# A hybrid diffusion layer on one core: last filter weights made at the modulation, bias frames moved, 24 convolution phases ahead of the attention

## The chip, the cores and the metric

The kernel runs on one core of a Trainium2 chip. The metric is the device time of one launch in microseconds (us): the median of several runs, and beside it one execution that the hardware profiler took, with its own time. The names of the engines are those of the profile: PE is TensorE (matmuls; PEld its weight loads), DVE is VectorE, ACT is ScalarE, POOL is GpSimd, and SP is SyncE, which here issues transfers only. Each engine, and each queue of transfers, works strictly in the order in which its instructions were written down.

## The reference

One layer is applied to 256 context tokens and 1024 latent tokens (a grid of 16 rows by 64) of width 1024, all in float32. Cut to what matters:

```python
h = _rmsnorm(x, norm1_g) * (1.0 + sc1) + sh1            # modulation, sc/sh from silu(c) @ w_ada + b_ada
proj = h @ w_in                                          # 1024 -> 3072 columns
q, k, v = heads(proj[..., :1536])                        # 8 heads of 64
hy = _dwconv3(proj[..., 1536:], hy_conv_w, hy_conv_b)    # three groups x1, x2, v of 512 channels
a = attend(q, k, v)                                      # latent: 8x16 neighbourhood + bias, and 256 context keys
z = x1 * _long_conv(v, k_f[:, 0], filt_bias[0])          # FFT convolutions, order 2
hyo = x2 * _long_conv(z, k_f[:, 1], filt_bias[1])
merged = concat(_rmsnorm(a, g_a), _rmsnorm(hyo, g_h))
x = x + g1 * (merged @ w_out)
u = _dwconv3(h2 @ w_up, ffn_conv_w, ffn_conv_b)          # then silu(gate) * up, @ w_down, residual, final norm
```

The filters of the long convolutions are themselves the output of a small network, whose last step is what the change touches:

```python
h = jnp.sin(freq * (z @ w1 + b1))
h = jnp.sin(freq * (h @ w2 + b2))
h = (h @ w3 + b3).reshape(L, HY_ORDER, 2, HY_CH)         # order, forward/backward, 512 channels
h = h * jnp.exp(-t[:, None] * deltas[None, :])[:, None, None, :]
k_f = rfft(concat(fwd, zeros, flip(bwd[1:])))
```

Outputs are the two token streams after the final norm and the context's keys and values.

## The kernel before

Products that need float32 accuracy are made of three matmuls (`mm3`, L115 to L118): each operand is split into a rounded high part (ACT, L121) and the rest (POOL, L122), and high x high, low x high and high x low are summed in PSUM. The program is written as Python that issues instructions; a scheduler sorts them by priority (normally the place where they are written) and by its own estimates, once, when the program is built. What runs is then fixed: one list for each engine and each queue. `tc.high_priority(offset=2000)` lets instructions compete as if written 2000 instructions earlier; `tc.issue_after(x)` forbids that a transfer or instruction is listed before x.

The stages, in the order of time:

1. **Modulation** (to 79 us). `filter_hidden` (L289) runs the two sine layers of the filter network. `adaln` (L210) streams the weights of scale and shift (tiles `wada`) through TensorE. Then, for three groups of tokens (`gi` 0, 1, 2: four, four and two tiles of 128 rows), tiles `x` are normalised (L511 to L514), transposed by TensorE (L267), scaled by ScalarE into `mo` (L269, L272), and split by VectorE into the high and low halves `hh` and `hl` (L274, L275), which stay in SBUF. The first query projection is made in the same loop, with its product in the PSUM tag `fA` (L533).
2. **Projections and filters** (80 to 560 us). 23 projections of 128 columns each (`proj`, L616) load a weight tile `wr` through SP (L606), split it and multiply it with all 1280 tokens into the PSUM tag `psp`. Twelve of them (`hy_chunk`, L652) feed the convolution and store transformed-ready tiles to DRAM (`lxd`, `cxd`); eleven (`qkv`, L682) feed the attention. Between their matmuls lie those of `filters` (L371): for each of the two orders, four blocks of 128 channels (`lat_filter`, L423) and the context's filter (`ctx_filter`, L470). One such block multiplies the hidden layer with the last weights (L376, PSUM tag `fB`), multiplies by the decays of ScalarE (`dec`, L380), corrects the first row with the filter bias (`fix0`, L382; its small load `fb`, L385, has one buffer), adds and subtracts on POOL (L394, L395), splits on ACT and DVE (L397, L399), transforms by `mm3` into `fA`, and stores to `Kd` or `Kc` in DRAM (L467, L489).
   The last weights of one order come from `w3load(o)` (L345): two loads of raw rows one after the other through the same buffer `csl0`, sums and differences into the buffer `cs0`, which the filters also use, and a split into `ws[0]` and `ws[1]`. It runs once in front of each order.
   `rpb_frames` (L550) makes one of three frames of the attention's position bias: 16 small transfers issued by POOL, a copy, a store to `rpw` in DRAM. The three are written behind the first three of the query, key and value projections (`j == 0`, L755).
3. **Convolution** (458 to 834 us). `chain(j)` (L772) convolves channel block j in two orders (j = 4 is the context). Each order has four *phases*, divided by `yield`: the forward transform (TensorE L805 into PSUM `cA`, ACT L813 to L818, DVE L819); butterflies and the product with the filter `K` loaded from `Kd` (DVE L826 to L847); inverse butterflies (DVE L852 to L857, ACT L862 and L863, DVE L864); and the inverse transform (TensorE L877, DVE L882 to L890). Two *lanes* run alternately, j = 0, 2, 4 in one and j = 1, 3 in the other, 40 turns in all (`turn2`, L903). The first 16 are written ahead of the attention, with three PSUM banks; the others are written into the attention, with one bank. The convolution uses the SBUF space of the filters, so it cannot begin before these are done.
4. **Attention** (598 to 866 us). POOL loads queries and keys of a head pair (`qkload`, L970), bias tables (`bias_load`, L958: 16 transfers from `rpw` for each of three tables `tb`) and values `vs` (L1044). `scores` (L1061) makes score products in PSUM `psS` (L1058), adds the bias and takes the maximum on DVE (L1079), and exponentiates on ACT (L1092, L1093). Then TensorE transposes the probabilities (L1102), ACT and DVE evict them (L1008, L1006), and TensorE multiplies with the values (L1016).
5. **Output projection, feed-forward** (from 866 us). The output weights `wor` are loaded and split (L1187, L1188) as soon as the convolution's buffers are free.

## Time and profile before

| | before |
|---|---|
| median of 3 runs | 1855.13 us (1854.43 to 1856.17) |
| the profiled execution: its own time | 1859.47 us |
| its span, first to last instruction | 1857.7 us |
| granted TensorE clock, mean | 0.962 |
| PE busy | 1723.9 us, 93% |
| DVE busy | 1368.3 us, 74% |
| ACT busy | 892.5 us, 48% |
| POOL busy | 396.3 us, 21% |

An engine's busy time is the union of its instructions. A row of a timeline gives the start and the length in us, engine, source line, operation, what is written and read, and in brackets how long the engine had been idle and what ended that. A row of busy time by stretch gives, for a stretch of the span, each engine's busy time with the number of its instructions. Matmuls overlap in TensorE's pipeline, so the distance from start to start, and not the length of one, tells how fast they follow each other. Lines below are those of the kernel before; in the changed kernel the lines behind L342 stand 6 to 18 lower.

### The profile page before, as it was taken

Reading aid. Unit: us, or ns where it says so; the run is one execution under the profiler, and the core shown is the slowest. Engines: PE = TensorE matmul, PEld = TensorE weight load, DVE = VectorE, ACT = ScalarE, POOL = GpSimd, SP = SyncE. Lnnn points to the kernel's source line nnn. Section 1 sums busy time; section 2 is a strip of 40 time slices with the busy share of each in tenths; the row PEclk is TensorE's granted clock in tenths of the full one; section 3 lists DMA queues with packets and bytes.
Section 4 is the critical chain, followed back from the end, with each engine's and each line's share of the span. In section 5 each row is a group of like instructions: output and inputs, shape, how many; then the busy total and the mean of one; then the engine's idle time right before and its main releaser. Section 6 shows DMA issues by size and latency. Waiting matters only on the chain.

```text
span 1857.7 us, 27350 instructions
## 1 busy us (share of the span) xinstructions
PE 1723.9 (93%) x9999; PEld 1453.9 (78%) x9999; DVE 1368.3 (74%) x2166; ACT 892.5 (48%) x1852; POOL 396.3 (21%) x487
## 2 busy tenths in 40 slices
PE   5899999999994689897998899999999999999997
PEld 1688778788783355465886899999999999788786
DVE  4668957861878789873467888889777877556797
ACT  4755545533333576664555444444444444443452
POOL 2366656673018325500110000000000000000001
PEclk7999999999996799898998999999999999999999
DMA  7424354356445323514331444555222122934653
GB/s 265 146 75 142 112 168 131 110 149 211 145 137 160 102 80 102 140 44 144 119 106 65 147 157 146 172 176 165 76 68 67 56 74 96 342 120 136 205 189 130
DMA packets 202438, 249.76 MB, mean 134 GB/s; under 512 B 21922, under 2 KB 147987, under 8 KB 202049
## 3 DMA queue, kind: packets, MB, share of 16 engines
q1 hardware_dynamic: 190360, 230.75, 38.5%
q0 software_dynamic: 10240, 16.46, 3.7%
q8 instruction: 78, 1.28, 0.3%
q10 hardware_dynamic: 1705, 0.82, 0.2%
q14 instruction: 55, 0.45, 0.1%
HBM read 176.75 MB, written 71.20 MB: 133 GB/s over the span
## 4 chain that ended last, share of the span: by engine, by line
PE 54%; DVE 19%; DMA 13%; ACT 5%; issue 5%; POOL 3%; SPq 0%; DVEq 0%; ACTq 0%; POOLq 0%
PE psd L116 5%; PE psd L117 5%; PE psd L118 5%; PE psp L116 4%; PE psp L118 4%; PE psp L117 4%; DMA wt<-in_w_down_dram 3%; PE psa L116 2%; PE psa L117 2%; PE psa L118 2%; DMA tdr<-wt 2%; PE psc L118 2%; PE psc L117 2%; PE psc L116 2%; PE psb L117 1%
## 5 line engine op out<-in xcount | busy, mean ns | idle before, releaser
L116 PE MATMUL psp<-hh,wh 128*128 128x512 f32 (+1 forms) x552 | 200.7, 364 | 1.9 <-ACT wh L121 1.9
L117 PE MATMUL psp<-hl,wh 128*128 128x512 f32 (+1 forms) x552 | 199.0, 361 | 0.0
L118 PE MATMUL psp<-hh,wl 128*128 128x512 f32 (+1 forms) x552 | 199.0, 361 | 0.0
L1737 POOL TENSOR_TENSOR rs<-rs,mhalf 128x1 f32<-128x1 f32 x10 | 7.7, 775 | 816.4 <-DVE rs L1736 816.4
L116 PE MATMUL psa<-T,ws 128*128 128x256 f32 (+1 forms) x528 | 165.8, 314 | 3.8 <-ACT rows L1536 2.7
L117 PE MATMUL psa<-T,ws 128*128 128x256 f32 (+1 forms) x528 | 165.1, 313 | 0.0
L118 PE MATMUL psa<-T,ws 128*128 128x256 f32 (+1 forms) x528 | 164.6, 312 | 0.0
L116 PE MATMUL psd<-wd,gs 128*128 128x512 f32 x360 | 140.7, 392 | 3.6 <-ACT gs L121 3.6
L117 PE MATMUL psd<-wd,gs 128*128 128x512 f32 x360 | 141.0, 392 | 0.0
L118 PE MATMUL psd<-wd,gs 128*128 128x512 f32 x360 | 123.8, 391 | 2.0 <-DVE gs L122 2.0
L116 PEld LDWEIGHTS psp<-hh,wh 128*128 128x128 f32 x552 | 104.9, 190 | 23.2 <-issue 7.4
L118 PEld LDWEIGHTS psp<-hh,wl 128*128 128x128 f32 x552 | 104.6, 189 | 15.3 <-issue 1.2
L117 PEld LDWEIGHTS psp<-hl,wh 128*128 128x128 f32 x552 | 104.9, 190 | 14.0 <-issue 0.4
L116 PE MATMUL psc<-T,ws 128*128 128x384 f32 (+1 forms) x352 | 110.0, 313 | 6.0 <-ACT ws L121 6.0
L967 POOL DMA_DIRECT2D tb<-rpw x192 | 100.3, 530 | 58.0 <-DVE m L1079 24.3
L117 PE MATMUL psc<-T,ws 128*128 128x384 f32 (+1 forms) x352 | 110.1, 313 | 0.0
L118 PE MATMUL psc<-T,ws 128*128 128x384 f32 (+1 forms) x352 | 109.7, 312 | 0.0
L117 PE MATMUL psb<-T,ws 128*128 128x384 f32 (+1 forms) x352 | 109.4, 311 | 0.0
L118 PE MATMUL psb<-T,ws 128*128 128x384 f32 (+1 forms) x352 | 109.4, 311 | 0.0
L116 PE MATMUL psb<-T,ws 128*128 128x384 f32 (+1 forms) x352 | 109.2, 310 | 0.0
L116 PEld LDWEIGHTS psa<-T,ws 128*128 128x128 f32 x528 | 101.3, 192 | 5.5 <-ACT rows L1536 3.9
L117 PEld LDWEIGHTS psa<-T,ws 128*128 128x128 f32 x528 | 101.3, 192 | 0.0
(404 smaller groups left out, 4783.9 us busy)
## 6 DMA issues: line engine op xcount, KB each, us to landing
wada<-in_w_ada_dram SPq DMA_DIRECT2D x48, 512.0 KB
wr<-in_w_up_dram SPq DMA_DIRECT2D x44, 512.0 KB
gr<-gdr SPq DMA_DIRECT2D x44, 320.0 KB
wr<-in_w_in_dram SPq DMA_DIRECT2D x23, 512.0 KB
wt<-in_w_down_dram SPq DMA_DIRECT2D x44, 256.0 KB
tdr<-wt SPq DMA_DIRECT2D x44, 256.0 KB
gdr<-cv SPq DMA_DIRECT2D x22, 512.0 KB
wr<-tdr SPq DMA_DIRECT2D x20, 512.0 KB
```

The costliest lines, as they stand in the source:

```text
L116: T.matmul(out, ah, bh, start=start, stop=False, skip_group_check=True)
L117: T.matmul(out, ah, bl, start=False, stop=False, skip_group_check=True)
L118: T.matmul(out, al, bh, start=False, stop=stop, skip_group_check=True)
L967: blast[0] = G.dma_start(out=tv[:, :, a * 8:a * 8 + 64], in_=rpw[var, :, 2 * p_:2 * p_ + 2, :, d * 8:d * 8 + 64].rearrange("q h u x -> q ( ...
L1737: G.tensor_tensor(rs, rs, mhalf, op=ALU.pow)
```

## The change

Five edits. `w3load(o)` is written for both orders inside the modulation, when the group `gi == 1` has its loads, together with the transform's table `dft`, `dlt` and `nt`, which stood behind the first `hy_chunk`; both halves of the raw rows get their own buffer, the difference moves from DVE to POOL, and POOL's results go straight to the rounded tiles, without a cast. The second order's pair is stored to DRAM (`W3d`) and loaded back in front of its filters. The bias frames move from `j == 0` to `j == 2`. The number of phases written ahead of the attention goes from 16 to 24. And the first loads of the attention get a forced order: first table, values, then the zeroing of the probability buffers and the other two tables.

```diff
-    W3GO = ()
     XW = (1,)
+    W3d = dr.tile([2, P, 1024], F32, name="W3d")
 
     def w3load(o):
+        cs = slice(o * 1024, (o + 1) * 1024)
+        raw = [ft([P, 2, 512], f"csl{i}") for i in range(2)]
+        w3 = I["filt_w3"][0, :, cs]
+        V.memset(raw[1][64:128], 0.0)
+        for i, q in ((0, 0), (0, 64), (1, 0)):
+            Q.dma_start(out=raw[i][q:q + 64].rearrange(f2), in_=w3)
+        for q in (64, 96):
+            Q.dma_start(out=raw[1][q:q + 1].rearrange(f2), in_=I["filt_b3"][0:1, cs])
+        s = ft([P, 2, 512], "csh0")
+        ws0 = ft([P, 2, 512], "GE" if o else "ws0", F32R)
+        for r, t in zip(raw, (ws0, s)):
+            G.tensor_add(t[:, 0], r[:, 0], r[:, 1])
+            G.tensor_sub(t[:, 1], r[:, 0], r[:, 1])
+        rd = ft([P, 2, 512], "csh1", F32R)
+        A.copy(rd, s)
+        ws1 = ft([P, 2, 512], "csl0" if o else "ws1", F32R)
+        G.tensor_sub(ws1, s, rd.bitcast(F32))
+        A.copy(ws1[64:96], rd[64:96].bitcast(F32))
+        if o:
+            for i, w in enumerate((ws0, ws1)):
+                Q.dma_start(out=W3d[i], in_=w.bitcast(F32).rearrange(f2))
+        return ws0, ws1
+
+    def w3again():
         ws = [ft([P, 2, 512], f"ws{i}", F32R) for i in range(2)]
...
+        for i, w in enumerate(ws):
+            Q.dma_start(out=w.bitcast(F32).rearrange(f2), in_=W3d[i])
         return ws
...
             if o:
-                Ws = w3load(o)
+                Ws = w3again()
...
                 with tc.issue_after(wlast) if gi else ExitStack():
-                    Q.dma_start(out=x, in_=src[0, row * P:(row + 1) * P])
+                    xlast = Q.dma_start(out=x, in_=src[0, row * P:(row + 1) * P]).ins
...
+            if gi == 1:
+
+                with tc.issue_after(xlast):
+                    t = ft([P, 512], "sd00")
+                    Q.dma_start(out=t, in_=I["t_dft"].flatten().rearrange("(p x) -> p x", p=P))
+                    split(t, dft[0].rearrange(f2), dft[1].rearrange(f2))
+                    Q.dma_start(out=dlt, in_=I["t_delta"])
+                    Q.dma_start(out=nt, in_=I["t_nt"])
+                    Ws0 = w3load(0)
+                    w3load(1)
...
             if j + which == 0:
...
-                with tc.issue_after(wloads[-1]):
-                    Ws0 = w3load(0)
                 filters(hs1, hs2, Ws0)
...
-            if j == 0:
+            if j == 2:
                 rpb_frames(ip.tile([P, LT], F32, tag="fo", name="rp", bufs=1), which)
...
     with tc.high_priority(offset=CHP):
-        phases(16)
+        phases(24)
...
     first = qkload(0)
-    for var in range(3):
-        G.memset(tbs[var], NEG)
-        bias_load(0, var)
-        if var == 0:
-            for r in Pring:
-                for t in r:
-                    G.memset(t[:, 0, :, 11:16], 0.0)
-                    G.memset(t[:, 1, :, 0:4], 0.0)
+    G.memset(tbs[0], NEG)
+    bias_load(0, 0)
+    with tc.issue_after(blast[0]):
+        vfirst, vlast = vload(0)
+    with tc.issue_after(vlast):
+        for r in Pring:
+            for t in r:
+                G.memset(t[:, 0, :, 11:16], 0.0)
+                G.memset(t[:, 1, :, 0:4], 0.0)
+        for var in (1, 2):
+            G.memset(tbs[var], NEG)
+            with tc.issue_after(blast[0]):
+                bias_load(0, var)
```

`vload` holds the three value loads that stood in `attend`, word for word.

How the scheduler moves the rest, at three places. First ACT at the end of the modulation, up to the cast of the first projection weights (`wh<-wr`); before:

```order
L269 ACTIVATE mo<-pstB,mods,A_79 128x256
L269 ACTIVATE mo<-psp,mods,A_79 128x256 x2
L272 ACTIVATE hh<-psp,mods,A_79 128x256
L269 ACTIVATE mo<-psp,mods,A_79 128x256
L269 ACTIVATE mo<-pstB,mods,A_79 128x256
L540 COPY tm<-psfA 128x256
L542 DMA qd<-tm 128x256
L121 CAST wh<-wr 128x1024
```

and in the changed kernel (`dec` are the filters' decays, `csh` the split of their sums, L423 the scaling behind their transform):

```order
L403 CAST csh_1011<-cs_1008 128x1024
L269 ACTIVATE mo<-psp,mods,A_79 128x256 x2
L272 ACTIVATE hh<-psp,mods,A_79 128x256
L386 ACTIVATE dec<-dlt,nt 128x128 x6
L269 ACTIVATE mo<-psp,mods,A_79 128x256
L386 ACTIVATE dec<-dlt,nt 128x128 x2
L269 ACTIVATE mo<-pstB,mods,A_79 128x256
L556 COPY tm<-psfA 128x256
L423 ACTIVATE tm<-psfA,tw 128x128 x2
L558 DMA qd<-tm 128x256
L121 CAST wh<-wr 128x1024
```

The filters of the first channel blocks have moved in between the modulation's own instructions, ahead of the first projection.

Second SP, the queue of the loads, at the same place; `fb` is the small filter bias, `wr` a projection's weights. Before:

```order
L221 DMA wada_0_2643<-in_w_ada_dram 128x1024
L216 DMA mr_2639<-in_b_ada_dram 4x256 x2
L606 DMA wr<-in_w_in_dram 128x8x128
L353 DMA csl_874<-in_filt_w_dram 64x1024
L744 DMA tm<-in_t_dft_dram 128x512
L355 DMA csl_874<-in_filt_w_dram 64x1024
L606 DMA wr<-in_w_in_dram 128x8x128 x2
```

and now:

```order
L368 DMA W3d<-GE 128x1024
L221 DMA wada_0_2646<-in_w_ada_dram 128x1024
L216 DMA mr_2642<-in_b_ada_dram 4x256 x2
L391 DMA fb<-in_filt_bias_dram 1x128
L368 DMA W3d<-csl_561 128x1024
L391 DMA fb<-in_filt_bias_dram 1x128 x2
L622 DMA wr<-in_w_in_dram 128x8x128 x5
```

The projections' weights now stand behind the stores of the second order's pair and behind three filter biases, the last of them that of the fourth channel block.

Third DVE at the first score (an ISA row is the maximum with bias, L1079 before and L1097 now). Before, these rows of the convolution stand just ahead of it:

```order
L826 TENSOR_TENSOR s_6035<-s_5773 128x1024
L864 SCALAR_TENSOR_TENSOR s_5623<-s_5623,tw,t 128x2x128
L827 TENSOR_TENSOR s_5773<-s_5773 128x4x256
L830 TENSOR_TENSOR s_6036<-s_6035 128x4x128
L831 TENSOR_TENSOR s_6036<-s_6035 128x4x128
L1079 ISA Pl_5833,m_5950<-psS,tb_5857 128x3x88
```

and now:

```order
L852 TENSOR_TENSOR s_6276<-s_6267,K 128x1024
L853 TENSOR_TENSOR s_6008<-s_6267,K 128x1024
L890 TENSOR_TENSOR tt<-pscA,s_6245 128x512
L891 TENSOR_TENSOR tt<-pscA,s_6245 128x512
L854 TENSOR_TENSOR s_6008<-s_6008,s_6276 128x512
L855 TENSOR_TENSOR s_6008<-s_6008,s_6276 128x512
L1097 ISA Pl_6068,m_6185<-psS,tb_6092 128x3x88
```

The convolution's lines stand 8 lower in the changed kernel, so L852 here is L844 of before. 155 of its instructions stood ahead of the first score on VectorE; now it is 240.

More of the change, by code (lines that the diff above doesn't have):

```diff
@@ L340, in _build @@
     f2 = "p a b -> p (a b)"
-    W3GO = ()
     XW = (1,)
+    W3d = dr.tile([2, P, 1024], F32, name="W3d")
     def w3load(o):
-        ws = [ft([P, 2, 512], f"ws{i}", F32R) for i in range(2)]
-        cs = slice(o * 1024, (o + 1) * 1024)
-        raw = ft([P, 2, 2, 512], "GO") if o in W3GO else None
-        for i in range(2):
-            r = raw[:, i] if o in W3GO else ft([P, 2, 512], "csl0")
-            s = ft([P, 2, 512], "cs0")
-            Q.dma_start(out=r[0:64].rearrange(f2), in_=I["filt_w3"][0, :, cs])
-            if i == 0:
-                Q.dma_start(out=r[64:128].rearrange(f2), in_=I["filt_w3"][0, :, cs])
-            else:
-                V.memset(r[64:128], 0.0)
-                for q in (64, 96):
-                    Q.dma_start(out=r[q:q + 1].rearrange(f2), in_=I["filt_b3"][0:1, cs])
-            G.tensor_add(s[:, 0], r[:, 0], r[:, 1])
-            V.tensor_sub(s[:, 1], r[:, 0], r[:, 1])
-            if i == 0:
-                A.copy(ws[0], s)
-            else:
-                rd = ft([P, 2, 512], "csh1" if o in W3GO else "csh0", F32R)
-                A.copy(rd, s)
-                G.tensor_sub(ws[1], s, rd.bitcast(F32))
-                A.copy(ws[1][64:96], rd[64:96].bitcast(F32))
@@ L740, in _build @@
             if j + which == 0:
-                t = ft([P, 512], "tm", bufs=2)
-                e = "p a b -> p (a b)"
-                Q.dma_start(out=t, in_=I["t_dft"].flatten().rearrange("(p x) -> p x", p=P))
-                split(t, dft[0].rearrange(e), dft[1].rearrange(e))
-                Q.dma_start(out=dlt, in_=I["t_delta"])
-                Q.dma_start(out=nt, in_=I["t_nt"])
-                with tc.issue_after(wloads[-1]):
-                    Ws0 = w3load(0)
                 filters(hs1, hs2, Ws0)
@@ L968, in bias_load, with vload @@
                     var, :, 2 * p_:2 * p_ + 2, :, d * 8:d * 8 + 64].rearrange("q h u x -> q (h u) x")).ins
+    def vload(p_):
+        vs = tp.tile([P, 12, P], F32, tag="vs", name="vs", bufs=2)
+        G.dma_start(out=vs[:, 0:10], in_=vd[:, :, p_ * P:(p_ + 1) * P].rearrange("n p x -> p n x"))
+        for h in range(2):
+            ld = G.dma_start(out=vs[:, 10:12, h * DH:(h + 1) * DH],
+                             in_=I["cache_ctx_v"][0, 0, 2 * p_ + h].rearrange("(n p) d -> p n d", p=P))
+        return vs, ld.ins
     def qkload(p_):
@@ L1041, in attend @@
             q, k = qkload(p_) if p_ else first
-        vs = tp.tile([P, 12, P], F32, tag="vs", name="vs", bufs=2)
         with tc.issue_after(blast0) if p_ == 1 else ExitStack():
-            G.dma_start(out=vs[:, 0:10], in_=vd[:, :, p_ * P:(p_ + 1) * P].rearrange("n p x -> p n x"))
-            for h in range(2):
-                G.dma_start(out=vs[:, 10:12, h * DH:(h + 1) * DH],
-                            in_=I["cache_ctx_v"][0, 0, 2 * p_ + h].rearrange("(n p) d -> p n d", p=P))
+            vs = vload(p_)[0] if p_ else vfirst
         if p_:
```

## The prediction, made before the changed kernel ran

> **What bounds the kernel now.** I read the page first, then busy time by stretch, then the stretches again for the convolution's buffers alone, then the timelines of VectorE and ScalarE at the seams. The columns after each stretch are its length and the busy time of PE, PEld, DVE, ACT and POOL, then granted clock, DMA share and GB/s.
>
> ```profile
> PE 1723.9 (93%) x9999; PEld 1453.9 (78%) x9999; DVE 1368.3 (74%) x2166; ACT 892.5 (48%) x1852; POOL 396.3 (21%) x487
> ...
> 46.00:80.00 34.00, 29.15 (x145) 20.38 (x143) 26.41 (x57) 28.32 (x47) 5.00 (x7) 0.95 0.50 157
> 80.70:458.00 377.30, 371.92 (x2298) 313.01 (x2299) 253.65 (x363) 179.49 (x376) 228.33 (x180) 0.99 0.45 134
> 467.00:598.00 131.00, 109.20 (x540) 87.62 (x539) 108.21 (x160) 49.49 (x145) 40.37 (x74) 0.90 0.48 142
> 598.00:866.00 268.00, 224.26 (x1334) 136.05 (x1334) 210.22 (x445) 161.36 (x494) 86.56 (x161) 0.92 0.36 103
> 725.00:866.00 141.00, 124.08 (x778) 76.31 (x774) 103.17 (x212) 88.15 (x251) 27.84 (x52) 0.96 0.34 99
> ```
>
> From 80.7 to 458 us (projections and filters) TensorE is busy 371.9 of 377.3 us: that stage ends when its matmuls end. In the stage before (46 to 80 us, the modulation) ScalarE is nearly full, 28.3 of 34.0. From 467 to 866 us nobody is full: TensorE idles 131.0 - 109.2 = 21.8 and then 268.0 - 224.3 = 43.7 us. What VectorE does there:
>
> ```profile
> 467.00:598.00 131.00, 35.46 (x120) 25.59 (x120) 105.00 (x150) 19.79 (x56) 0.90 0.48 142
> 598.00:725.00 127.00, 25.58 (x84) 17.35 (x84) 70.66 (x103) 12.18 (x34) 0.88 0.39 107
> 725.00:866.00 141.00, 25.35 (x100) 17.47 (x100) 50.11 (x74) 11.82 (x28) 0.96 0.34 99
> ...
> 459.97 0.48 DVE L819 SCALAR_TENSOR_TENSOR s<-pscA,tw,t 128x256 f32<-128x256 f32 x1 [14.60 <-ACT t L818]
> 549.24 1.22 DVE L844 TENSOR_TENSOR s<-s,K 128x1024 f32<-128x1024 f32 x1 [5.15 <-DMA K<-Kd]
> 585.75 0.48 DVE L819 SCALAR_TENSOR_TENSOR s<-pscA,tw,t 128x256 f32<-128x256 f32 x1 [3.58 <-ACT t L818]
> 597.77 0.42 DVE L1079 CUSTOM_DVE_ANT_0 Pl<-psS,tb 128x264 f32<-128x264 f32 x1
> ```
>
> The first three rows count only instructions on the convolution's buffers s: 105.0 of VectorE's 108.2 us up to 598, 70.7 + 50.1 = 120.8 of its 210.2 afterwards; in all 225.8 us for 327 of them, and 86.4 of TensorE for 304. The first score (L1079, 597.8 us) carries no wait: VectorE, in order, comes to it only when the convolution ahead of it is done. So the attention starts when VectorE has worked through the phases put first, and the question is what it costs to put more there, and when they can start.
>
> **The change part by part.** The sum is made against the profiled execution, 1859.5 us.
>
> Part 1, modulation, +17. In the order of the program ScalarE now gets, before the cast of the first projection weights: 24 decays, a table load, six casts of 128x1024 or 32x1024, one of 128x512 (half of that) and two small scalings, 0.8 together as an estimate from the 0.3 of a decay.
>
> ```profile
> 20.73 1.28 ACT L380 ACT_TABLE_LOAD   x1
> 22.03 1.57 ACT L380 ACTIVATE dec<-dlt,nt 128x128 f32<-128x128 f32 x5
> 24.94 1.28 ACT L329 ACT_TABLE_LOAD   x1
> 24.29 0.41 DVE L326 TENSOR_SCALAR sd<-sd 64x512 f32<-64x512 f32 x1
> 79.62 1.04 ACT L121 CAST wh<-wr 128x1024 fp32r<-128x1024 f32 x1 [0.42 <-ACT tm L540]
> 94.67 1.05 ACT L368 CAST ws<-csh 32x1024 fp32r<-32x1024 f32 x1 [2.50 <-POOL ws L367]
> ```
>
> 24 x 0.314 + 1.28 + 6 x 1.05 + 0.6 + 0.8 = 16.5 us, on an engine that has 34.0 - 28.3 = 5.7 us of gaps, which are waits on VectorE and stay. At the front the two table loads and eight decays leave ScalarE, but the sine behind them also needs L326, which ends at 24.70, so only 26.24 - 24.70 = 1.5 is won; with the 0.25 MB of dlt gone from the head of the queue I take -2. The cast moves from 79.6 to 94.1. The wait that is added: on SP the first five projection loads (one at 67.7 before) now stand behind the filter bias of the fourth channel block, which waits for VectorE's correction of the third, four VectorE rows before the modulation's last; TensorE waits for those loads. Bounds: a load of this size took from its issue at 38.41 to ScalarE's start at 45.87 behind other loads, 7.5; ScalarE's last rows cover 2 to 3 of that; so 0 to 5, and I take 2.5.
>
> ```profile
> 38.41 0.54 SPq L523 DMA_DIRECT2D cs<-in_w_in_dram  x1
> 45.87 1.06 ACT L525 ACTIVATE GO<-cs 128x1024 fp32r<-128x1024 f32 x1 [6.10 <-DMA cs<-in_w_in_dram]
> 67.73 0.43 SPq L606 DMA_DIRECT2D wr<-in_w_in_dram  x1
> ```
>
> Sum 16.5 - 2 + 2.5 = +17. Bounds: -2 (the filters' front part fits the other engines' gaps) and +22.
>
> [...] The rows first: L845, 1.22 us alone, took 3.41 while GpSimd's split ran from 498.10 to 501.45, itself longer than the 2.38 it takes with VectorE idle.
>
> ```profile
> 481.02 1.22 DVE L845 TENSOR_TENSOR s<-s,K 128x1024 f32<-128x1024 f32 x1
> 499.12 3.41 DVE L845 TENSOR_TENSOR s<-s,K 128x1024 f32<-128x1024 f32 x1
> 498.10 3.35 POOL L122 TENSOR_TENSOR wl<-wr,wh 128x1024 fp32r<-128x1024 f32 x1 [33.16 <-DVE mr L229]
> 80.75 2.38 POOL L122 TENSOR_TENSOR wl<-wr,wh 128x1024 fp32r<-128x1024 f32 x1 [14.70 <-ACT wh L121]
> ```
>
> [...] What that does to this stage is a rival below.
>
> Part 2, the convolution can start earlier, -67. Before, the first convolution matmul (about 458 us) comes after 18 of the 23 projections, now after 14: filters begun in the modulation, the second order's weights only loaded, and the bias frames' 48 issues no longer among the filters' adds on GpSimd.
>
> ```profile
> 379.72 0.39 PE L116 MATMUL psp<-hh,wh 128*128 128x512 f32 x1
> 379.94 0.39 PE L117 MATMUL psp<-hl,wh 128*128 128x512 f32 x1
> 384.48 0.28 PE L116 MATMUL psp<-hh,wh 128*128 128x256 f32 x1
> 384.59 0.28 PE L117 MATMUL psp<-hl,wh 128*128 128x256 f32 x1
> ...
> L556 POOL DMA_DIRECT2D rp<-in_rpb_dram x48 | 29.6, 620 | 0.9 <-POOL rp L552 0.9
> ```
>
> Between the first projection and the first convolution matmul the order holds 192 fewer 512-wide and 157 fewer 256-wide ones (95 projection, 44 filter, 18 transform). By their start-to-start spacing, 0.2275 (mean of the neighbours; the first two rows round to 0.22) and 0.12, that is 43.7 + 18.8 = 62.5; counted so, the whole stage makes 349 where it took 377, so -67. The 29.6 us of bias frames lie on GpSimd, which from then on has nothing that is waited for; without that cover they would delay the first bias table. The frames, tables and values for the first pair now land ahead of a score that VectorE reaches late anyway: 0.
>
> Part 3, 24 phases first, +76. VectorE's order holds 155 convolution instructions before the first score, now 240: 85 x 105.0/150 = 59.5 us, and five others that the longer stretch takes in, 2.9 by L845-like sizes. VectorE was busy 108.21/131 = 0.826 of this stretch; the gaps are the loads of K and ScalarE's scaling, which come once per phase. 62.4/0.826 = +76. Bounds: 62 (no gap) and, at the pace quoted next, far more.
>
> ```profile
> 540.00:560.00 20.00, 17.80 (x92) 15.14 (x91) 14.17 (x22) 5.70 (x17) 1.94 (x3) 1.00 0.57 191
> ```
>
> TensorE has room: its 109 us there grow by the 62.5 of part 2 and 33 x 86.4/304 = 9.4, to 181 of 207. First score: 598 + 17 - 67 + 76 = 624.
>
> Part 4, the attention loses those phases, -38. Lower bound TensorE's 9.4; upper bound VectorE's 85 x 225.8/327 = 58.7 at its 210.22/268, 75. Between them by parts: the order ends the convolution at 84 of 144 score rows, near 725 us of before. Behind it 25.35 of TensorE's 124.08 go but 2; where nothing disturbs it, a turn (four transposes, four products) follows the next without a gap:
>
> ```profile
> 840.17 0.66 PE L1102 MATMUL psX<-ident,Pl 128*128 128x128 f32 x4
> 840.76 0.65 PE L1016 MATMUL psav<-pt,vs 128*64 128x256 f32 x4
> 841.34 0.66 PE L1102 MATMUL psX<-ident,Pl 128*128 128x128 f32 x4
> ```
>
> so 101/0.95 = 106 for 141, or 115 at today's share of 0.88; I take 111, -30. Ahead of it VectorE keeps 92 x 0.69 = 63.5 of 70.7: -7/0.84 = -8.
>
> Part 5, output weights, -1. They are split earlier, since the convolution's buffers come free. At the end ScalarE's square waits behind such a split:
>
> ```profile
> 865.42 0.72 ACT L1187 ACTIVATE wh<-wor,vec 128x512 fp32r<-128x512 f32 x1 [0.78 <-DMA wor<-in_w_out_dram]
> 866.05 1.04 ACT L1212 ACTIVATE sq<-at 128x1024 f32<-128x1024 f32 x1
> ```
>
> 0.6 us directly; bounds 0 and 4. Everything after is unchanged.
>
> Sum: 17 - 67 + 76 - 38 - 1 = -13, 1846.5. The profiled execution stands 4.3 above the median of the runs, 1855.1; predicted 1842.
>
> **Rivals.**
> A, slower: VectorE's pace under projections. 240 instructions behind bursts of projection matmuls run like 540 to 560 us, 14.17 of 20 busy. 170.6/0.71 = 240 instead of 207: 1876. It decides from the point where the added stretch is 89, a pace of 0.775. For it: the K loads sit in SP's queue behind projection loads. Against: 467 to 598 was mostly under projections and held 0.826.
> B, slower: the attention is TensorE's. Only the 9.4 comes off: 1842 + 29 = 1871. For it: TensorE is its busiest engine. Against: 43.7 us idle.
> C, much faster: the attention is VectorE's, -75: 1805. For it: 107 of 127 us up to 725. Against: 103 of 141 behind.
> D: the filters' front fits into the gaps of the modulation, part 1 near 0: 1825. For it: VectorE and GpSimd have room; against it ScalarE's full row.
> E: VectorE locked out in the modulation. GpSimd gets eight adds of half a buffer, one split of that size and two of full size there, each at or half of the 2.38 of the quoted split, together about 15.5 us. If VectorE stood still for all of it, its 26.4 us, with about 12 of filter work added, would become 54; ScalarE's 34.0 + 16.5 = 50.5 was the bound, so +3.5: 1845. For it: the rows of 499 us. Against: one engine's gaps absorb part of it. [...]
> F: start and end cancel, no measurable change: 1855.
>
> **How the numbers follow.** Forecast 0.37 (1828 to 1852), A 0.13, B 0.10, C 0.14, D 0.13, E 0.06, F 0.07. Faster by over 0.2%, about what a measurement of this kernel can tell from no change (1851.4): forecast, C, D, E but their edge, 0.67; slower (1858.8): A and B, 0.23; within 0.10. Parts 1 and 2 are uncertain by about 6 each, 3 and 4 by about 15, together 22; the range 1812 to 1870 leaves out most of C and the far ends of A and B. The forecast's own range is 1828 to 1852.
>
> **What would show it.** Right: the first projection matmul near 97 us, the first convolution matmul near 408, the first score near 624 with VectorE about 0.83 busy before it, the convolution finished well before the attention, which ends near 853 after some 230 us. Wrong: projections that start by 82 or after 105; VectorE below 0.775 between first convolution and first score; attention still 255 us or longer; or TensorE under 0.95 busy between projections and convolution, which would mean that the denser filters stall it.

## The result, and the profile after

The changed kernel is slower: 1887.8 us (1886.1 to 1890.8) beside 1855.2 (1854.4 to 1856.2) of the kernel before, a ratio of 1.0177 (95% interval 1.0160 to 1.0195). Predicted were 1842, with a range of 1812 to 1870. Its profiled execution took 1890.8 us, with a span of 1889.0; the one of before took 1859.5.

| us in the profiled executions | before | predicted | after |
|---|---|---|---|
| first projection matmul | 80.7 | 97 | 105.5 |
| first convolution matmul | 457.9 | 408 | 419.9 |
| last projection matmul | 560 | | 596 |
| first score on VectorE | 597.8 | 624 | 629.5 |
| end of the attention | 865.4 | 853 | 894.6 |
| first score to end of the attention | 267.6 | 230 | 265.1 |
| behind it, to the end of the span | 992.3 | | 994.4 |

The end of the attention is that of the last row that writes `at` on VectorE. So up to the first score the forecast was 5.5 us too early. The attention was to give 38 back and gave 2.5. That is where most of the 46 us of error stands in the traces; the runs below show that the cause begins earlier.

The page of the changed kernel, busy time and granted clock (compare the page's rows in the prediction):

```profile
PE 1738.2 (92%) x9999; PEld 1467.9 (78%) x9999; DVE 1380.0 (73%) x2162; ACT 888.1 (47%) x1848; POOL 411.0 (22%) x491
```

TensorE is 14.3 us busier than before, with the same matmuls. Busy time by stretch, modulation, projections with filters, the convolution under projections, the stretch with no projection, and the attention in two parts (columns as in the prediction: length, PE, PEld, DVE, ACT, POOL, granted clock, DMA share, GB/s):

```profile
43.70:105.50 61.80, 45.84 (x209) 35.11 (x208) 50.19 (x76) 44.41 (x82) 32.27 (x24) 0.80 0.41 126
105.50:420.00 314.50, 302.52 (x1891) 255.62 (x1892) 231.41 (x331) 151.69 (x324) 183.01 (x124) 0.98 0.44 135
420.00:596.00 176.00, 175.46 (x948) 146.93 (x947) 146.89 (x217) 72.28 (x198) 50.47 (x62) 1.00 0.54 165
596.00:629.50 33.50, 15.98 (x50) 10.53 (x49) 25.26 (x42) 11.46 (x40) 29.22 (x62) 0.67 0.64 172
629.50:759.00 129.50, 102.82 (x532) 61.89 (x532) 90.23 (x200) 68.22 (x223) 50.33 (x95) 0.82 0.33 91
759.00:894.60 135.60, 116.14 (x739) 67.63 (x735) 68.63 (x164) 77.67 (x219) 32.12 (x60) 0.92 0.25 74
```

and the same for the kernel before, from its first score, up to the first score of the third head pair and from there to the end:

```profile
597.80:713.70 115.90, 89.35 (x487) 52.73 (x489) 95.95 (x208) 67.29 (x228) 49.83 (x93) 0.87 0.37 103
713.70:865.40 151.70, 134.40 (x849) 82.81 (x845) 114.44 (x239) 93.50 (x267) 36.50 (x69) 0.97 0.36 102
```

Three things are to be seen. From 420 to 596 us TensorE is busy 175.46 of 176: no matmul of the convolution goes into a gap there, each pushes the projections back. VectorE lost a quarter of its work in the attention (210.4 to 158.9 us), and the attention is as long as it was. And both parts of the attention changed by what TensorE's busy time changed: the first is 13.6 longer with TensorE 13.5 busier, the second 16.1 shorter with TensorE 18.3 less busy.

The modulation, timelines of GpSimd and VectorE of the changed kernel: twice a row of GpSimd and the row of VectorE that runs beside it, and then the same two rows of VectorE when they run alone:

```profile
58.62 1.72 POOL L359 TENSOR_TENSOR csh<-csl 128x512 f32<-128x512 f32 x1
59.12 1.77 DVE L275 TENSOR_TENSOR hl<-mo,hh 128x512 fp32r<-128x512 f32 x1
66.73 2.79 POOL L364 TENSOR_TENSOR ws<-csh,csh 128x1024 fp32r<-128x1024 f32 x1
67.31 2.50 DVE L274 CAST hh<-mo 128x512 fp32r<-128x512 f32 x1
62.34 0.69 DVE L275 TENSOR_TENSOR hl<-mo,hh 128x512 fp32r<-128x512 f32 x1
74.81 0.41 DVE L274 CAST hh<-mo 128x512 fp32r<-128x512 f32 x1
```

A cast of 0.41 us takes 2.50 while GpSimd's difference runs, and a difference of 0.69 takes 1.77 beside GpSimd's sum; they end 0.29 and 0.55 us behind these rows of GpSimd. The row of VectorE that the prediction quoted for this, L845 (3.41 us for 1.22), has two inputs; the cast has one.

### The profile page after: what moved, and what is told of

Its sections match the earlier page's. It is cut to its first block, busy times and chain, and to the rows that moved or that the text cites. A ratio compares the mean times of both kernels' runs of the same rounds, so it can differ in the third digit from the quotient of the medians.

```text
span 1889.0 us, 27373 instructions
## 1 busy us (share of the span) xinstructions
PE 1738.2 (92%) x9999; PEld 1467.9 (78%) x9999; DVE 1380.0 (73%) x2162; ACT 888.1 (47%) x1848; POOL 411.0 (22%) x491
## 4 chain that ended last, share of the span: by engine, by line
PE 48%; DVE 13%; DMA 10%; ACT 4%; issue 4%; POOL 2%; SPq 0%; DVEq 0%; POOLq 0%; ACTq 0%
PE psd L116 6%; PE psd L118 6%; PE psd L117 6%; PE psa L116 2%; PE psa L117 2%; PE psa L118 2%; DMA wt<-in_w_down_dram 2%; PE psav L1038 2%; PE psX L1120 2%; PE psc L118 2%; PE psp L116 2%; PE psc L117 2%; PE psc L116 2%; PE psp L117 2%; PE psp L118 2%
```

## The experiments

All ratios are against the kernel before, run beside it on the same chip; where us are given for a run as its total they are its ratio times 1855.2. The other columns are from the profiled executions, in us: the last projection matmul, the first score, the end of the attention, the distance between these two, its mean granted clock, and that distance times that clock ("full clock"), a rough measure of how long it would be at full speed. In the expectations P stands for the terms of the prediction and T for the view that TensorE's own list sets both the first score and the length of the attention. Names with b_ start from the kernel before, those with x_ from the changed one.

| run | ratio (95%) | last projection | first score | end of attention | attention | clock | full clock |
|---|---|---|---|---|---|---|---|
| before | 1 | 560 | 597.8 | 865.4 | 267.6 | 0.92 | 246 |
| changed | 1.0177 (1.0160 to 1.0195) | 596 | 629.5 | 894.6 | 265.1 | 0.87 | 231 |
| b_mod | 1.0061 (1.0046 to 1.0077) | 583 | 607.5 | 869.8 | 262.3 | 0.93 | 244 |
| b_frames | 0.9998 (0.9981 to 1.0014) | 563 | 599.1 | 865.8 | 266.7 | 0.94 | 251 |
| b_order | 0.9934 (0.9914 to 0.9954) | 561 | 598.3 | 848.8 | 250.5 | 0.94 | 235 |
| b_rpb | 0.9930 (0.9906 to 0.9953) | 560 | 596.5 | 844.8 | 248.3 | 0.94 | 233 |
| x_phases16 | 1.0038 (1.0022 to 1.0055) | 584 | 607.9 | 867.5 | 259.6 | 0.94 | 244 |
| x_nomod | 1.0145 (1.0128 to 1.0162) | 562 | 652.8 | 892.0 | 239.2 | 0.96 | 230 |
| x_phases40 | 1.0308 (1.0273 to 1.0342) | 596 | 709.4 | 921.9 | 212.5 | 0.92 | 196 |
| b_ph12 | 0.9982 (0.9969 to 0.9995) | 563 | 595.6 | 859.8 | 264.2 | 0.94 | 248 |
| x_tabfirst | 1.0122 (1.0095 to 1.0149) | 596 | 629.5 | 890.6 | 261.1 | 0.87 | 227 |
| x_tabonce | 1.0133 (1.0110 to 1.0155) | 597 | 629.8 | 891.8 | 262.0 | 0.88 | 231 |
| x_sq | 1.0164 (1.0149 to 1.0179) | 595 | 629.3 | 889.4 | 260.1 | 0.89 | 231 |
| b_sq | 0.9949 (0.9935 to 0.9964) | 562 | 598.4 | 855.7 | 257.3 | 0.95 | 244 |
| x_noav | 1.0037 (1.0020 to 1.0055) | 599 | 631.5 | 872.1 | 240.6 | 0.89 | 214 |
| x_w3dve | 1.0042 (1.0025 to 1.0058) | 598 | 627.3 | 869.7 | 242.4 | 0.94 | 228 |
| x_w3dve16 | 1.0053 (1.0037 to 1.0069) | 585 | 611.2 | 875.5 | 264.3 | 0.93 | 246 |
| x_twice | 1.0117 (1.0102 to 1.0132) | 596 | 628.7 | 882.8 | 254.1 | 0.93 | 236 |
| b_twice | 0.9939 (0.9916 to 0.9962) | 564 | 601.3 | 859.2 | 257.9 | 0.97 | 250 |

### Each edit alone

`b_mod` is the kernel before with the first edit only (the hunks of `w3load`, `w3again` and the modulation). `b_frames` moves only the bias frames, `b_order` only forces the order of the attention's first loads, `b_rpb` does both.

```diff
-            if j == 0:
+            if j == 2:
                 rpb_frames(...)
```

> The kernel before with the first edit alone: last weights made at the modulation, with the transform's table; frames, loads and 16 phases as before. P (the prediction's parts 1 and 2: 17 later into the projections, 67 earlier into the convolution, and the first score follows the convolution): first score near 548, 1805. T (the first score cannot come before TensorE has ended the projections, and 24 us of first loads behind them; TensorE has the same work to the end of the projections and starts it 25 later): projections end at 584, first score 608 to 615, 1863 to 1880.

> The kernel before with the bias frames moved behind the filters and nothing else. With both the frames moved and the first loads forced, 13 us came off, all in the attention (267.6 -> 248.3; the first score and the convolution's start did not move). If the frames do it: 1846 within 4. If the forced order of the first loads does it: 1857 within 4.

> The kernel before with the forced order of the attention's first loads alone. The frames alone measured 0.9998 of before, both together 0.993. If the order does it without the frames: 1844 within 5. If it needs the frames out of the way: 1857 within 4.

> The kernel before with only two of the five edits: bias frames behind the filters and the first loads of the attention in forced order; 16 phases, last weights in front of each order. P (the prediction gave both edits no cost of their own and part of the earlier convolution): convolution starts some 15 us earlier, total 1840 to 1855. T (the first score waits for the end of the projections plus the attention's first loads): projections end at 560 as before, first score 584 to 598, total 1845 to 1857.

The first edit alone costs 11 us (0.61%) where the prediction's parts 1 and 2 made it 50 faster. Its convolution starts at 417 instead of 458, as foreseen, and the first score comes at 607.5, not 548. The stretches of `b_mod` from the convolution's start to the last projection, and on to the first score:

```profile
417.40:583.20 165.80, 164.87 (x897) 137.60 (x896) 132.57 (x191) 67.14 (x182) 43.95 (x49) 1.00 0.54 165
583.20:607.50 24.30, 13.65 (x55) 8.99 (x53) 5.76 (x14) 7.74 (x28) 23.68 (x53) 0.79 0.64 157
```

VectorE, which the prediction took to set the first score, is busy 5.76 of the last 24.3 us. TensorE was full up to the last projection, and behind it its list holds transposes that wait for a load, then a convolution step, then the scores:

```profile
594.87 0.66 PE L748 MATMUL pstB<-ident,ck 128*128 128x128 f32 x2 [5.95 <-DMA ck<-in_cache_ctx_k_dram]
596.80 2.04 PE L813 MATMUL pscA<-s,dftf 128*128 128x256 f32 x4 [1.28 <-DMA s<-lxd]
600.35 2.07 PE L813 MATMUL pscA<-s,dftf 128*128 128x256 f32 x4 [1.51 <-DVE s L827]
602.36 2.21 PE L1066 MATMUL psS<-k,q 64*128 64x264 f32 x8
```

The projections start 24.4 later than before and end 23 later. So the earlier convolution was paid for by TensorE, and the 24 us of the modulation went through almost in full.

The frames alone do nothing (0.9998), and do not move the convolution's start either. The forced order of the first loads, to which the prediction gave nothing, is worth 12 us alone (0.9934), all of it in the attention (267.6 to 250.5). Its first pair takes 59.1 us instead of 70.1, with 49 of VectorE's convolution instructions in it instead of 63. What in the changed list does that was not followed further.

### How many phases ahead

```diff
-        phases(24)
+        phases(16)
```

This is `x_phases16`; `x_phases40` has 40 there, `x_nomod` is the changed kernel without its first edit, and `b_ph12` is `b_rpb` with 12 phases.

> The changed kernel with 16 phases ahead of the attention instead of 24; all else as in the changed kernel (1887.8 us; first score 629.5, attention 265.1 us from first score to its last product). P (the terms of the prediction): the 8 phases cost 76 ahead of the first score and 38 in the attention, so first score near 553, attention near 303, 1850. T (TensorE's own work sets both): it was busy 175.46 of the 176 us from 420 to 596 us, so projections still end near 587 and the first score cannot come before some 590; the attention is as long with the 8 phases in it as without, 265 to 270; 1887.8 - 40 + 3 = about 1851. The totals agree, the first score (553 or 590) and the attention (303 or 268) tell the two apart.

> The changed kernel with the filter network's last weights made in front of each order again, as in the kernel before; bias frames, 24 phases and forced first loads stay. Both theories: first projection back near 81, first convolution matmul near 455. P (prediction): first score near 598 + 76 = 674, the attention 38 shorter than before's 267.6, so 1855.2 + 38 = 1893. T: with only five projections behind 458 us TensorE has no cover for the added phases, first score near 670, and the attention stays at 265: 1855.2 + 72 = about 1927.

> The changed kernel with all 40 phases written ahead of the attention, so hardly any convolution is left in it. P (the prediction's part 4, the attention gives back about half of what stands ahead): 16 phases cost about 70 before the first score and give 50 to 60 back, attention near 210, total near 1900. T (the convolution lies in the attention's gaps nearly for free): attention 240 to 255 even without it, total 1935 or more.

> The kernel before with frames moved and first loads forced (0.993 of before), and 12 phases ahead of the attention instead of 16: the opposite direction of the change. Per convolution instruction of VectorE, 0.87 us ahead of the first score and 0.12 to 0.57 inside the attention were found. If the marginal price inside stays below the one ahead: four phases fewer take up to 20 to 30 off ahead and give 5 to 20 back, 1825 to 1840; but the first score cannot come before the projections' end at 560 and 24 us of loads, so at most 12 earlier, then 1838 to 1850.

Phases 17 to 24 can be priced three times, in pairs of kernels that differ in nothing else (differences in us; the third pair is described below):

| 16 and 24 phases | total | first score | attention |
|---|---|---|---|
| with the first edit: `x_phases16`, changed | +26 | +21.6 | +5.5 |
| without it: `b_rpb`, `x_nomod` | +40 | +56.3 | -9.1 |
| sums on VectorE: `x_w3dve16`, `x_w3dve` | -2 | +16.1 | -21.9 |

The prediction's parts 3 and 4 had +38, from +76 and -38. So the price depends on the rest of the list, and in the third pair the phases cost nothing that could be told from zero. Four phases fewer than 16 cost 10 (`b_ph12`, 0.9930 to 0.9982), since the first score, at 595.6, came only 0.9 earlier for them; its total, 1852, lies just outside the 1838 to 1850 expected for that case.

`x_phases16` scores at 607.9, where T had put it (590 at the earliest) and not at 553; its total, 1862, is 11 above what either had. In the other two runs P was nearer than T. `x_nomod` took 1882 (P 1893, T 1927): its first score came at 652.8, earlier than both had it, and its attention shrank to 239.2, where T had it unchanged. That the same 24 phases leave 265.1 us in one kernel and 239.2 in the other had to be explained. `x_phases40` took 1912 (P 1900, T 1935 or more), with 212.5 us of attention and no convolution in it:

```profile
709.40:921.90 212.50, 178.82 (x1148) 101.70 (x1148) 100.64 (x270) 127.77 (x390) 82.27 (x154) 0.92 0.26 66
```

So the convolution is not free in the attention. But TensorE is busy 0.84 of it (178.82/212.50), as in the attentions that are full of convolution (223.75/267.60 before, 218.96/265.10 after, both the sums of the rows above), and the 52.6 us that came off go with the 40.1 that TensorE lost.

### The loads on GpSimd's queue

The trace showed a suspect. GpSimd's queue between the second and third pair, changed kernel:

```profile
735.01 0.98 POOL L980 DMA_DIRECT2D vs<-vd  x1 [21.89 <-PE psav L1038]
735.98 1.42 POOL L982 DMA_DIRECT2D vs<-in_cache_ctx_v_dram  x2
737.39 2.63 POOL L975 DMA_DIRECT2D tb<-rpw  x5
740.87 15.68 POOL L975 DMA_DIRECT2D tb<-rpw  x30 [0.84 <-DMA vs<-vd]
756.71 5.75 POOL L975 DMA_DIRECT2D tb<-rpw  x11 [0.17 <-issue]
```

The values wait for a buffer, and 46 table loads wait behind them. `x_tabfirst` puts the tables first, `x_tabonce` leaves the tables of pairs 1 to 3 out (they keep those of pair 0, so their bias is wrong), `x_sq` also takes the squares out of the query buffer, and `b_sq` does what `x_sq` does in `b_rpb`.

```diff
-            vs = vload(p_)[0] if p_ else vfirst
+            vs = vload(p_)[0] if p_ == 1 else vfirst
         if p_:
             ...
+        if p_ > 1:
+            with tc.issue_after(blast[0]):
+                vs = vload(p_)[0]
...
-            sq = asq if p_ == 0 else tp.tile([P, LT], F32, tag=f"q{p_ % 2}", name="sq", bufs=1)
+                    sq = tp.tile([P, 512], F32, tag="bs", name="sq", bufs=2)[:, :n]
```

> The changed kernel with the values of head pairs 2 and 3 loaded behind their 48 bias-table loads on GpSimd's queue instead of ahead of them. Q (GpSimd's queue holds the attention: the value load waits for the products of two pairs before, 21.9 and 28.1 us, and the table loads, 0.53 us each, stand behind it): the gaps between the pairs' maxima, 742.2 to 759.0 and 804.7 to 827.9, close to a few us each, and up to TensorE's idle time there, 85.7 - 71.1 = 14.6, or somewhat more as its clock holds, comes off: about 1870. T (TensorE's transposes and products hold it): the maxima move, the end does not, 1888 within 4.

> The changed kernel, in which head pairs 1 to 3 keep the bias tables of pair 0 (their 144 table loads are left out, so the bias of these pairs is the wrong one). Takes the whole chain of table loads away. Q: at least what the reordered loads gain, 15 to 35: 1853 to 1873. T: 1888 within 4. If it gains clearly more than the reordered loads, the number of loads and not only their place is a limit.

> The changed kernel with the values of pairs 2 and 3 loaded behind their tables and, new, the squares of the finished pairs made in three pieces in the small buffers of the reciprocals instead of in the query buffer of the pair after next. In the run with only the tables first the queries of pair 3 waited 38.3 us on GpSimd's queue for that square, and 40 table loads stood behind them; in the run without any table loads they waited too. Q (GpSimd's queue, through whichever wait stands first in it, holds the last pairs): the distance from the end of pair 1's second half to the first maximum of pair 3, 37.3 us (790.6 to 827.9), falls to 10 to 15 or so, attention 265 -> 240 to 250, total 1863 to 1873. T (TensorE's transposes and products take that time anyway): the maxima come earlier, the end moves less than 8, as with the tables alone.

> The same two edits of the attention's loads in the kernel with only the bias frames moved and the first loads forced, 16 phases (0.993 of before; there the end of pair 1 to the first maximum of pair 3 took 45.3 us, 731.8 to 777.1). Q: another 10 to 20 off, 1825 to 1834. T: 1844 within 5.

The suspect explains little. Tables first gained 10 us (1.0177 to 1.0122) and no tables at all 8, between what the two views had forecast, and the version with both waits gone 2; in `b_rpb` it lost 4. In `x_tabfirst` the wait only moved to the next load in the queue:

```profile
805.45 0.57 POOL L988 DMA_DIRECT2D q<-qd  x1 [38.32 <-DVE asq L1179]
```

and where that too was gone, in `x_sq`, the first maximum of the last pair still came at 821.1 instead of 827.9. Long waits on a queue, named as such by the profile, were worth at most 10 us when they were taken away. Why `x_sq` lost most of what tables first had gained was not followed.

### TensorE's share

`x_noav` leaves out the products of the local probabilities with the values, so its attention is that of the context keys alone.

```diff
                 for vt, ps in local(cb):
-                    av_mm(av, 256 * j, vt, ps, False)
+                    pass
```

> The changed kernel without the products of the local probabilities with the values (56 groups of four matmuls are left out; the transposes before them and all else stay), so the attention's output is that of the context keys alone. One group takes 0.65 us when nothing disturbs it, 36 us in all. T (TensorE's own in-order work sets the attention's length): the attention, 265.1 us, shrinks by 25 to 36, 1852 to 1863. L (it is the chain of score, maximum, exponential and eviction, or GpSimd's loads, with TensorE waiting for them): at most 10 off, 1878 or more.

```profile
631.50:872.10 240.60, 182.28 (x1043) 118.23 (x1041) 158.48 (x362) 144.67 (x441) 82.28 (x154) 0.89 0.33 91
```

TensorE's busy time falls by 36.7, the attention by 24.5, the kernel by 26 us (1.0177 to 1.0037), with VectorE's work unchanged. So of a microsecond taken from TensorE two thirds come off here, while a quarter of VectorE's work went for 2.5 us and 144 table loads for 8. The attention goes mainly with TensorE's work, but not at a fixed share: TensorE is busy 0.83 to 0.89 of it in the kernels with the whole attention, and 0.76 here.

### The clock

With 24 phases ahead, the last column of the table is 227 to 231 in the six kernels with the whole attention and no added work; with 16 phases it is 233 to 251. Where only the phases differ it falls by 13 (with the first edit), 3 (without) and 18 (sums on VectorE). By this measure the phases did come off the attention, and in the changed kernel the lower clock took about as much back: 265.1 x (0.92 - 0.87) = 13. That is arithmetic with a mean clock; it does not show that the clock is the cause. The first pair of the changed kernel, and that of `x_w3dve`, a run described below:

```profile
629.50:710.90 81.40, 57.40 (x252) 34.02 (x252) 60.83 (x121) 36.13 (x121) 26.26 (x50) 0.74 0.38 112
```

```profile
627.30:692.60 65.30, 50.77 (x255) 31.32 (x255) 53.67 (x115) 35.11 (x115) 29.91 (x56) 0.84 0.52 147
```

Three matmuls fewer keep TensorE busy for 6.6 us more at 0.74 than at 0.84. VectorE also has 7.2 us more to do in the longer one. To tell cause from companion, `x_twice` gives TensorE more to do: the convolution's matmuls in the first pair are issued twice with the same operands.

```diff
-                    for i in range(2):
+                    for i in list(range(2)) * twice[0]:
                         T.matmul(pa[...], dftf[:, i, hs], uv[:, i, xs], start=True, stop=True)
...
+        twice[0] = 2 if p_ == 0 else 1
         for n, _ in enumerate(attend(p_)):
```

> The changed kernel, in which the convolution's matmuls that are written into the first head pair (about 56, 28.6 us of TensorE there) are issued twice with the same operands, so TensorE has more to do and fewer gaps; the result is the same. K (TensorE's granted clock, 0.74 over the first pair, falls in its gaps, and the low clock is what makes this attention 265 long where the run without the first edit took 239 at 0.96): the clock over the first pair rises to 0.85 or more, and the doubled work costs less than half its time, total within 6 of the changed kernel. W (the gaps only follow from VectorE's and the loads' pace, the clock costs nothing there): the doubled matmuls add 14 to 28, total 1900 or more.

> The kernel before with the forced order of the first loads (0.9934 of before) and the convolution's matmuls in the first head pair issued twice, as it was done in the changed kernel, where it took 11 us off. K (the granted clock of the first pair is what the added matmuls raise; here it is already 0.82 instead of 0.74, and 40 matmuls of the convolution, about 19 us, lie in that pair): the clock goes to about 0.9, 0 to 6 off, 1838 to 1844. W (added work costs its time): 6 to 15 more, 1850 or above.

```profile
628.70:882.80 254.10, 216.76 (x1308) 132.83 (x1308) 159.30 (x364) 145.87 (x442) 82.16 (x154) 0.93 0.31 88
628.70:701.50 72.80, 52.98 (x267) 34.49 (x269) 54.69 (x116) 33.36 (x114) 26.18 (x50) 0.88 0.38 110
```

With 41 more matmuls in the attention (1308 instead of 1267) TensorE is busy 216.8 us instead of 219.0, the clock of the first pair is 0.88 instead of 0.74, and the kernel is 11 us faster (1.0117). In the kernel with the forced loads the doubling, 48 matmuls, neither gains nor loses (0.9939 beside 0.9934; the profiled execution of `b_twice`, 1851.0 us, stands 6.6 above its median), although the clock there was higher, 0.89 from 597.0 to 656.5 us, than in the first pair of `b_order`, 0.82 from 598.3 to 657.4. That the added work cost nothing that could be measured is shown in both. That the clock brought the 11 us is not: the lists moved as well, and the first pair of `x_twice`, 8.6 us shorter, holds 6.1 us less of VectorE's work (60.83 to 54.69), with 59 of its convolution instructions instead of 64. `x_nomod` leaves the same choice open. Its attention is 26 us shorter than the changed kernel's, all of it in the first pair: 49.0 us instead of 81.4 (the other three are 6.5 longer), at a clock of 0.90, and with 44 of those instructions:

```profile
652.80:701.80 49.00, 38.97 (x212) 24.23 (x213) 43.19 (x99) 32.17 (x113) 26.14 (x50) 0.90 0.36 94
```

So a first pair with less of VectorE's convolution in it is a rival to the clock, and no run takes the two apart. In the rows quoted here for the changed kernel the clock is 1.00 where TensorE is busy 175.46 of 176.00 us, 0.74 at 57.40 of 81.40 and 0.67 at 15.98 of 33.50; in the first pair of `x_twice` it is 0.88 at 52.98 of 72.80. What sets it was not shown.

### GpSimd beside VectorE

`x_w3dve` makes the ten sums and differences of the last weights on VectorE; `x_w3dve16` is the same with 16 phases.

```diff
-            G.tensor_add(t[:, 0], r[:, 0], r[:, 1])
-            G.tensor_sub(t[:, 1], r[:, 0], r[:, 1])
+            V.tensor_add(t[:, 0], r[:, 0], r[:, 1])
+            V.tensor_sub(t[:, 1], r[:, 0], r[:, 1])
...
-        G.tensor_sub(ws1, s, rd.bitcast(F32))
+        V.tensor_sub(ws1, s, rd.bitcast(F32))
```

> The changed kernel with the ten sums and differences of the last weights on VectorE instead of GpSimd. L (GpSimd's rows hold VectorE's casts and two-input rows for their whole length; the rows that are too long add up to some 15 us, 11 of them beside these ten): VectorE pays 8 x 0.69 + 2 x 1.22 = 8.0 itself and loses 11 of waiting, its casts of 128x512 are back at 0.41 until the filters' own sums begin; first projection 105.5 -> about 102, total 1885 within 3. S (ScalarE's added 16.5 us bound that stage, as the prediction had it): first projection stays at 105 or goes later by VectorE's 8 us, 1888 to 1896.

> The changed kernel with the last weights' sums on VectorE and 16 phases. Both single changes took about 26 us off the changed kernel. If they are independent: 1836. If both remove the same stall in the attention: 1860. C (the phases put first cost, the earlier start of the convolution is worth something only where VectorE is late): the first score comes 10 to 15 behind the last projection's 24, near 605, the attention 245 to 250, 1848.

In the modulation what L expected came. VectorE's casts are back to their length:

```profile
61.91 0.68 DVE L360 TENSOR_TENSOR GE<-csl 128x512 fp32r<-128x512 f32 x1
62.51 0.42 DVE L274 CAST hh<-mo 128x512 fp32r<-128x512 f32 x1
62.91 1.21 DVE L364 TENSOR_TENSOR ws<-csh,csh 128x1024 fp32r<-128x1024 f32 x1
```

and the first projection comes at 101.0 instead of 105.5, although VectorE has ten more rows. The total fell far more than L had it, by 25 us (1.0042). The 4.5 do not explain that. They do not even reach the last projection, at 597.1 instead of 595.8, and with 16 phases the same edit gains nothing (1.0053 beside 1.0038), so that `x_w3dve16`, at 1865, lies above all three totals expected of it. Nor does the earlier convolution, which starts at 399 instead of 420 us here, and with 16 phases at 400 instead of 418. What differs with 24 phases is the attention, 242.4 instead of 265.1: its first pair, with 57 of VectorE's convolution instructions in it instead of 64, takes 65.3 us instead of 81.4, at 0.84 of the clock instead of 0.74. Which of these does how much was not taken apart.

## Why the prediction was wrong, point by point

**What bounds the kernel.** "So the attention starts when VectorE has worked through the phases put first" is the sentence that failed. It was true of the kernel before, where VectorE was 38 us behind the last projection, and not of one whose convolution starts 40 us earlier. There TensorE's list decides, through the last projection and 24 us of loads, transposes and convolution steps behind it (`b_mod`: 583 to 607.5). The row that said so was quoted and not used: TensorE busy 371.9 of 377.3 us means that what is moved into that stage is not free, and in `b_mod` 23 of the 24.4 us put ahead of it came out behind it.

With eight more phases in front, the changed kernel has VectorE last again. Its first score carries no wait:

```profile
629.49 0.42 DVE L1097 CUSTOM_DVE_ANT_0 Pl<-psS,tb 128x264 f32<-128x264 f32 x1
```

It missed the forecast by only 5.5 us, in part by luck: parts 1 and 2 came out 7.8 and 4.2 us too long, and the way from the first convolution matmul to the first score 6.3 shorter than part 3 had it (+69.7 for +76). So in the changed kernel's own trace the term that missed is part 4: the attention was to give back 38 us and gave 2.5, 35.5 of the 45.8 us of error. Two of the prediction's signs of being wrong came, projections that start after 105 (105.5) and an attention of 255 us or longer (265.1); VectorE at 0.82 and TensorE at 0.96 were not among them.

**Part 1, +17.** Measured +24.8. ScalarE's sum was right (28.3 to 44.4 us busy, +16.1 beside 16.5). That its gaps stay was not: 5.7 us became 17.4 (61.80 - 44.41). Of the missing 7.8, 4.5 come off when GpSimd's ten sums go to VectorE (`x_w3dve`). That fits rival E, which had 3.5 for it; but GpSimd's rows are also longer themselves (1.72 us for a sum that took 0.68 on VectorE), and the two were not separated. The wait for the projections' weights, 2.5 in the sum, was 0.5 at ScalarE's cast (104.38 us). The rest was not taken apart.

**Part 2, -67.** The size was nearly right: 377.2 to 314.4 us from the first projection to the first convolution matmul, -62.8, all of it by the first edit, none by the frames. Its worth was wrong. Parts 1 and 2 together were to be -50; the edit alone measured +11. This is the largest error, 61 us, and it stands in the step that passed the earlier start on to the first score. Along the runs the change is +11 (first edit), then -4 (frames and loads, which were -13 without the first edit), then +26 (phases), together +33; the prediction had -50, 0 and +38.

**Part 3, +76, and part 4, -38.** Together +38. Measured, +26 with the first edit, +40 without it and -2 in `x_w3dve`. As terms both failed. VectorE's pace was right (172.2 us busy of 209.5 from the convolution's start to the first score, 0.82 for 0.826), so the first score came near the forecast. But against a kernel that waits for TensorE anyway (607.9) it moved by 21.6 and not by 76, and the attention gave back nothing (259.6 to 265.1).

In part 4 two things went wrong, seen with the attention cut at the first score of its third pair, 11 us before the cut of the prediction. Behind the middle "101/0.95 = 106 for 141" let TensorE's share rise to 0.95 once the convolution is gone; it stayed at 0.86 (116.14/135.60), and there were -16 instead of -30. Ahead of it stood -8, and it became +13.6: 45 matmuls more in that part, 23 of them the convolution's, and a clock of 0.82 instead of 0.87. Full turns without gaps, as in the three rows quoted for it, are not what a whole pair looks like. Why the attention gave nothing back, the clock or VectorE's work in its first pair, stays open. The instructions on the convolution's buffers in these two parts, two rows of before and two of the changed kernel:

```profile
597.80:713.70 115.90, 23.48 (x76) 15.98 (x76) 63.21 (x93) 10.33 (x29) 0.87 0.37 103
713.70:865.40 151.70, 27.46 (x108) 18.84 (x108) 57.60 (x86) 13.67 (x33) 0.97 0.36 102
629.50:759.00 129.50, 31.45 (x99) 20.23 (x97) 55.51 (x81) 13.19 (x33) 0.82 0.33 91
759.00:894.60 135.60, 5.25 (x20) 3.46 (x20) 8.03 (x13) 0.67 (x2) 0.92 0.25 74
```

So 65 matmuls of the convolution left the attention (184 to 119). The prediction's lower bound, "33 x 86.4/304 = 9.4", counted half of them; at its own rate it would have been 18.5.

**Part 5, -1.** 11.8 us from the end of the attention's last product to the first matmul of the output projection became 11.3. Right.

**The rivals.** B was nearest in mechanism: the attention is TensorE's, and mainly what leaves TensorE comes off. Its price rested on the 9.4 us above. The convolution's matmuls there did fall, by 14.2 us, but TensorE's busy time fell by only 4.8, at a lower clock, and the attention by 2.5. "43.7 us idle", the argument against B, was no argument: 27 to 46 us of idle time are there in every kernel with the whole attention. A, VectorE's pace, did not happen. It was also priced alone, as 34 us on top of the forecast, and not as a sign that the steps before it rest on the same wrong idea of who waits for whom.

## What to carry to other kernels

Where an engine is full for a whole stage, expect work put ahead of that stage to come out behind it (23 of 24.4 us in `b_mod`), and work moved into it to push its end back (the last projection from 584 to 596 us with eight more phases); an earlier start of something else is worth nothing until one has checked what its first consumer waits for in the new order. Do not let an engine's share of busy time rise in a forecast because a competitor leaves: here TensorE's was 0.83 to 0.89 with the convolution in the attention and 0.84 without. Take the single edits apart before shipping a bundle: here one was worth 12 us, one nothing, one cost 11, and the phases cost 40, 26 or nothing, as the rest of the list had it.

## What the runs showed of the hardware

Work added on TensorE was free, or better, here: with 41 matmuls added to an attention its busy time there was 2.2 us lower, while the granted clock of the first pair was 0.88 instead of 0.74. On VectorE a cast, with a single input, took 2.50 us beside a difference on GpSimd and 0.41 alone; a difference, with two, took 1.77 beside a sum on GpSimd and 0.69 alone. And a version better than both kernels came out: the kernel before with only the forced order of the first loads, 0.9934 (0.9914 to 0.9954), some 12 us.
